# Reading the gate and up products later, behind the next weight tile's split, in a mixture-of-experts stage

## The chip, the core and the metric

The program runs on one core of one Trainium2 chip. The metric is the device time of one execution in microseconds (us), the median of the runs shown; shorter is better. In the profile the core's engines are named PE (matrix products; PEld is its weight load), DVE (element-wise work), ACT (element-wise work with a scale or a function), POOL and SP (which here issues the loads from device memory).

## What is computed

Two layers of a decoder trunk over 272 positions of width 1024, in f32. Each has three token mixers; then layer 0 has a dense SwiGLU block, and layer 1 a mixture of 8 experts, of which every token uses 2. Only the last part is touched here:

```python
def swiglu(h, w_gate, w_up, w_down):
    return (jax.nn.silu(h @ w_gate) * (h @ w_up)) @ w_down

def moe_swiglu(h, router_w, w_gate, w_up, w_down):
    logits = jnp.einsum('btd,de->bte', h, router_w).astype(jnp.float32)
    top_logits, top_idx = lax.top_k(logits, TOP_K)
    ...
    for e in range(N_EXPERTS):
        out = out + combine[..., e:e + 1] * swiglu(h, w_gate[e], w_up[e], w_down[e])
```

The gate and up weights of an expert are 1024 x 3584, the down weights 3584 x 1024, all f32: 44 MB for each expert and 352 MB for the eight.

## The kernel before

The first 850 us or so are the mixers of both layers and the dense block. Then comes the stage of the experts, `experts` (L1162), which is what the change touches.

**Tokens and experts.** The experts are ranked by how many tokens they got. The four fullest are "wide" (up to 128 tokens each), the others "narrow" (up to 64). A token block is gathered by a product with a one-hot matrix (`Group.gather`, L1000) and kept as two parts whose sum is the f32 value: a rounded one and a rest.

**Weights.** An expert is worked through in 7 chunks of 512 hidden columns. A chunk needs 6 loads of 1 MB, in this order: two halves of the gate weights (names r_g), two of the up weights (r_u), two of the down weights (r_d). Every loaded tile is split as a whole (`MoveWeights.parts`, L847): ACT writes the rounded part h_g, h_u or h_d (L855), then DVE the rest, l_g, l_u or l_d (L856). There are 6 raw tiles (`RB`) and 4 pairs of split tiles (`HB`): a load waits until DVE has split the tile six before it, a split waits until PE has used the part four before it. From here on "part" is one such split tile.

**Products.** For each 128 rows of weights a wide expert needs three products of 128 x 512 (L1106 to L1108), a narrow one two (L1134, L1135), since its two halves of tokens stand side by side. A part is 12 products for a wide chunk, 8 for a narrow one. The gate products gather in psg, the up products in psu (two accumulators, `pg`), the down products in y.

**Reading psg and psu.** In a wide chunk ACT reads psg as h (the SiLU, in `act`, L78) and DVE multiplies h by psu (L1113). In a narrow one ACT copies psg to gs (L1140) and psu to us (L1141). Then `turn` brings the result into the layout that the down products need: PE transposes it into hps (L1120, and L1149 for a narrow chunk, gs and us by 8 small products each). In a wide chunk ACT then writes hth (L1124) and DVE htl (L1125). In a narrow one ACT makes s (the SiLU, L78), DVE multiplies it (L1152), and ACT and DVE write ht (L1155, L1156). The down products of a chunk are issued one chunk later: `gate_up` of a chunk, with the `turn` of the chunk before in its middle (`between`), then `down` of the chunk before (`finish`).

**Order.** The list at L1225 to L1231 puts four wide chunks first, then narrow and wide ones by turns, and the three narrow ones that are left last. When an expert's last chunk is done, its sum is weighted (yh, yl) and added to the output (`combine`). SP issues the loads in the order of the program. On the other engines a scheduler sets the order of the instructions: it places each by what it depends on and the estimated times, and the program can add an order between two instructions that share no data (`tc.add_manual_dep` with `nosync`: no wait, only a place behind the other, on the same engine). Each engine then works through its queue strictly in order.

Of the kernel before, what the change touches and what calls it, by code (L numbers as in the profile page):

```python
# [9 lines left out]
F32 = mybir.dt.float32  # L10
# [4 lines left out]
AF = mybir.ActivationFunctionType  # L15
ALU = mybir.AluOpType
# [3 lines left out]
P = 128  # L20
# [31 lines left out]
def trunk(ctx: ExitStack, tc: tile.TileContext, x, meta, n1g, n2g, w_in, qng, kng, dlam,  # L52
# [3 lines left out]
    V, A, G, PE = nc.vector, nc.scalar, nc.gpsimd, nc.tensor  # L56
# [6 lines left out]
    nosync = mybir.DependencyInfo(mybir.DependencyClass.NoSync, mybir.DependencyReason.DATA)  # L63

    def raw_ins(i):
        return getattr(i, "ins", i)
# [9 lines left out]
    def act(*args, **kw):  # L76

        i = raw_ins(A.activation(*args, **kw))  # L78
        for b in phase["before"]:
            tc.add_manual_dep(i, b.name, nosync, reason="tables")  # L80
        phase["now"].append(i)
        return i
# [34 lines left out]
    with ExitStack() as lctx:  # L117
# [16 lines left out]
        def ptile(name):  # L134
            return pm.tile([P, 512], F32, tag="pm", name=name)
# [63 lines left out]
        for k in range(KD):  # L199
            tps = pp.tile([P, 512], F32, tag="pp", name="xT")  # L200
            PE.transpose(tps[:, 0:NM], min_[:, k * P:(k + 1) * P], ident[0:NM, 0:NM])
            for t in range(2):
                c = NM + t * P
# [147 lines left out]
        for l in range(2):  # L351
# [226 lines left out]
            for hp in range(0, NH, 2):  # L578

                lgs = {}  # L580
                for X in (TA, TB):
# [5 lines left out]
                    for m in range(2):  # L587
                        b = m * 2 + hp // 2
                        pss = [ptile("lgps") for _ in range(2)]
# [189 lines left out]
            for fp in range(NFD // 2):  # L779
# [3 lines left out]
                for j in range(2):  # L783
                    pss = []
# [8 lines left out]
                    gs, us, sg = ft[:, 0, :], ft[:, 1, :], ft[:, 2, :]  # L793
# [32 lines left out]
    mo = ctx.enter_context(tc.tile_pool(name="mo", bufs=1, **MT))  # L826
# [7 lines left out]
        return pw.tile([P, 512], F32, tag="pw", name=name)  # L834

    nparts = [0]
    EARLY = 3

    class MoveWeights:
# [7 lines left out]
        def parts(self):  # L847
            st = min(2048 // self.cols, self.nk)
            for k0 in range(0, self.nk, st):
                late = nparts[0] % HB >= HB - LATE  # L850
                wq, nb_ = (wqs[0], LATE) if late else (wqs[1], HB - LATE)
                hi = wq.tile([P, st, self.cols], F32R, tag="hi", bufs=nb_, name="h_" + self.name)
                lo = wq.tile([P, st, self.cols], F32R, tag="lo", bufs=nb_, name="l_" + self.name)
                r = self.raw[:, k0:k0 + st, :]
                ih = raw_ins(A.activation(hi, r, AF.Copy))  # L855
                il = raw_ins(V.tensor_tensor(lo, r, hi.bitcast(F32), op=ALU.subtract))  # L856
                nparts[0] += 1
                if EARLY < nparts[0] < 9:

                    tc.add_manual_dep(il, routed[0].name, nosync, reason="router")  # L860
                if EARLY < nparts[0] < 9:
                    tc.add_manual_dep(ih, last_in[0].name, nosync, reason="router")
                for k in range(st):
                    yield k0 + k, hi[:, k, :], lo[:, k, :]

# [156 lines left out]
    class Expert:  # L1022
# [9 lines left out]
        def gate_up(self, c, between):  # L1032
            pss = []
            for nm, m in (("g", m_wg), ("u", m_wu)):
                ps = pg.tile([P, 512], F32, tag="pg", name="ps" + nm)
                for kh_ in range(2):
                    w = MoveWeights(self.src(m, slice(kh_ * 512, kh_ * 512 + 512), slice(c * 512, c * 512 + 512)),
                                    4, 512, f"{nm}{c}_{kh_}")
                    for kk, hi, lo in w.parts():
                        k = kh_ * 4 + kk  # L1040
                        self.products(ps, [self.g.x[:, k, s] for s in self.sides], hi, lo, k == 0, k == KD - 1)
                pss.append(ps)
                if nm == "g":
                    between()
            return self.gated(*pss)

        def down(self, c, ht):
            if c == 0:
# [52 lines left out]
    class Wide(Expert):  # L1101
# [5 lines left out]
            PE.matmul(ps, st[0], lo, start=False, stop=False)  # L1107
            PE.matmul(ps, st[1], hi, start=False, stop=last)  # L1108

        def gated(self, psg, psu):  # L1110
            h = mo.tile([P, 512], F32, tag="h", bufs=2, name="h")
            act(h, psg, AF.Silu, scale=self.g.ws[:, 0, 1:2])
            V.tensor_tensor(h, h, psu, op=ALU.mult)  # L1113
            return h

        def turn(self, h):

# [10 lines left out]
    class Narrow(Expert):  # L1128
# [5 lines left out]
            PE.matmul(ps, st[0], hi, start=first, stop=False)  # L1134
            PE.matmul(ps, st[0], lo, start=False, stop=last)  # L1135

        def gated(self, psg, psu):
            gs = mo.tile([P, 512], F32, tag="h", bufs=2, name="gs")
            us = mo.tile([P, 512], F32, tag="hu", bufs=2, name="us")
            A.activation(gs, psg, AF.Copy, scale=self.g.ws[:, 1, 1:2])  # L1140
            A.activation(us, psu, AF.Copy)  # L1141
            return gs, us

        def turn(self, gu):
            hps = wtile("hps")
# [16 lines left out]
    def experts(groups, order, first=None):  # L1162


        made, xs = {}, {}
        todo = []

        def group(gi):
            w, n = groups[gi]
            made[gi] = Group(w, n, oh0 if first and gi == 0 else one_hot(w, n, pos_s, sel_s))  # L1170

        def short(n=1):
            for _ in range(min(n, len(todo))):
                todo.pop(0)()

        def finish(x, c, ht):
            if c == NCE - 1:
                ct = x.combine_turn()
            x.down(c, ht)
            if c == NCE - 1:  # L1180
                todo[0:0] = x.combine(ct)

        starts = {}
        for i, (gi, q, kind, c) in enumerate(order):
            starts.setdefault(gi, i)
        group(0)
        for k in range(KD):
            made[0].gather(k)
        if first:
            new_phase("silu_and_others")  # L1190
        prev = None
        for i, (gi, q, kind, c) in enumerate(order):
            for gj, at in starts.items():
                if at == i + (2 if first and gj == 1 else 3):
                    group(gj)
                    todo.extend([lambda g=made[gj], k=k: g.gather(k) for k in range(KD)])
                if at == i and i:
                    short(len(todo))
            if (gi, q) not in xs:
                xs[gi, q] = kind(place[q], made[gi])  # L1200
                xs[gi, q].last = False
            x = xs[gi, q]
            x.last = i == len(order) - 1
            ht = []

            def between():
                if not hasattr(made[gi], "ws"):
                    made[gi].weights()
                short(2 if len(todo) > 4 else 1)
                if prev is not None:  # L1210
                    ht.append(prev[0].turn(prev[2]))
            if first and i == 1:
                residual(1)
            h = x.gate_up(c, between)
            short(2 if len(todo) > 4 else 1)
            if prev is not None:
                finish(prev[0], prev[1], ht[0])
                short()
            prev = (x, c, h)
        finish(prev[0], prev[1], prev[0].turn(prev[2]))  # L1220
        short(len(todo))

# [6 lines left out]
    for i in range(len(narrow)):  # L1229
        order.append(narrow[i])  # L1230
        order.extend(wide[LAG + i:LAG + i + 1])  # L1231
    experts([(0, None)] + [(q, q + WIDE - 1) for q in range(1, WIDE)] + [(None, NE - 1)], order, True)

    cnt = nc.values_load(cmaxi[0:1, 0:1], min_val=0, max_val=S + P // 2)
# [34 lines left out]
```

## Time and profile before

| | us |
|---|---|
| median of 3 runs | 1889.6 |
| lowest and highest run | 1888.64, 1890.66 |
| the profiled execution | 1889.8 |
| its span, first to last instruction | 1888.0 |
| PE busy in the span | 1764.2 (93%) |
| DVE busy | 1438.7 (76%) |
| ACT busy | 1140.0 (60%) |

Busy shares are averages over stages that differ. For the experts one reads the stretch from about 880 us on: first how busy each engine and the DMA engines are there, then which waits there are and what ends them, then the engines' work in order of time for one pair of chunks, a wide one and a narrow one. A wait is idle time of an engine, with the instruction whose end released it. An instruction that waits holds up all that stands behind it in its engine's queue.

### The profile page before, as it was taken

To read this page: it belongs to the slowest core of one execution; us is meant where nothing else is said; L and a number is where in the kernel's file an instruction comes from. 1 tells how busy PE (TensorE), PEld (TensorE's weight loads), DVE (VectorE), ACT (ScalarE), POOL (GpSimd) and SP (SyncE) were. 2 spreads that over 40 slices of the span, in tenths; PEclk is the share of its full clock that TensorE was granted. 3 is DMA by queue.
4 is the path that set the end of the run, shared out by engine and by line. 5 is a ranking of instruction groups with operands and counts; after the bars stand their busy time and mean duration, and the time that the engine had idled before them with its cause. 6 is when DMAs were issued, how large, how long until landed. Compare 5 with 4: busy or idle time off the path is not lost.

```text
span 1888.0 us, 27076 instructions
## 1 busy us (share of the span) xinstructions
PE 1764.2 (93%) x10613; PEld 1523.0 (81%) x10613; DVE 1438.7 (76%) x1600; ACT 1140.0 (60%) x1253; POOL 114.3 (6%) x137
## 2 busy tenths in 40 slices
PE   7999999999999999999998899898899989989986
PEld 7888999999998889998776677676677666767764
DVE  7667657877575776687888788887878878888886
ACT  4376444444443754466776677676677767677765
POOL 5201101000002020020000000000000000000000
PEclk9999999999999999998999999999999999999999
DMA  6333555455553336576999999999999998999994
GB/s 209 100 92 92 179 177 178 158 179 173 174 173 106 109 103 191 187 281 219 342 364 359 314 343 356 344 354 319 343 334 353 359 351 321 356 348 351 365 336 174
DMA packets 266117, 479.91 MB, mean 254 GB/s; under 512 B 7637, under 2 KB 115229, under 8 KB 265981
## 3 DMA queue, kind: packets, MB, share of 16 engines
q1 hardware_dynamic: 265472, 477.20, 72.8%
q8 instruction: 85, 1.39, 0.3%
q0 software_dynamic: 368, 0.86, 0.1%
q14 instruction: 52, 0.42, 0.1%
q10 hardware_dynamic: 140, 0.04, 0.0%
HBM read 477.01 MB, written 1.05 MB: 253 GB/s over the span
## 4 chain that ended last, share of the span: by engine, by line
PE 39%; DVE 14%; ACT 8%; issue 5%; POOL 0%; ACTq 0%; DVEq 0%; POOLq 0%
DVE l_d L856 4%; ACT h_d L855 4%; DVE l_g L856 4%; DVE l_u L856 3%; PE psg L1107 3%; PE psg L1108 2%; PE psg L1106 2%; PE psu L1135 2%; ACT h_g L855 2%; PE y L1107 2%; ACT h_u L855 2%; PE proj L229 2%; PE proj L230 2%; PE proj L228 2%; PE y L1108 2%
## 5 line engine op out<-in xcount | busy, mean ns | idle before, releaser
L856 DVE TENSOR_TENSOR l_d<-r_d,h_d 128x2048 fp32r<-128x2048 f32 (+1 forms) x114 | 256.1, 2250 | 84.8 <-ACT h_d L855 84.8
L230 PE MATMUL proj<-hgh,lo_in 128*128 128x272 f32 (+1 forms) x1024 | 297.5, 291 | 4.6 <-DVE lo_in L224 4.6
L228 PE MATMUL proj<-hgh,hi_in 128*128 128x272 f32 (+1 forms) x1024 | 298.2, 291 | 0.2 <-DVE z L357 0.2
L229 PE MATMUL proj<-hgl,hi_in 128*128 128x272 f32 (+1 forms) x1024 | 296.5, 290 | 0.0
L856 DVE TENSOR_TENSOR l_u<-r_u,h_u 128x2048 fp32r<-128x2048 f32 x112 | 254.6, 2287 | 52.5 <-ACT h_u L855 52.4
L856 DVE TENSOR_TENSOR l_g<-r_g,h_g 128x2048 fp32r<-128x2048 f32 x112 | 255.5, 2286 | 19.0 <-ACT h_g L855 19.0
L223 ACT ACTIVATE hi_in<-raw_in 128x1024 fp32r<-128x1024 f32 x128 | 135.0, 1058 | 166.0 <-PE proj L229 150.6
L855 ACT ACTIVATE h_g<-r_g 128x2048 fp32r<-128x2048 f32 x112 | 213.5, 1910 | 11.6 <-PE psu L1108 6.9
L855 ACT ACTIVATE h_u<-r_u 128x2048 fp32r<-128x2048 f32 x112 | 211.2, 1907 | 12.9 <-PE y L1108 6.5
L855 ACT ACTIVATE h_d<-r_d 128x2048 fp32r<-128x2048 f32 (+1 forms) x114 | 212.3, 1877 | 4.8 <-PE psg L1108 2.5
L230 PEld LDWEIGHTS proj<-hgh,lo_in 128*128 128x128 f32 x1024 | 194.0, 189 | 6.5 <-DVE lo_in L224 5.5
L228 PEld LDWEIGHTS proj<-hgh,hi_in 128*128 128x128 f32 x1024 | 194.1, 190 | 2.8 <-issue 1.1
L229 PEld LDWEIGHTS proj<-hgl,hi_in 128*128 128x128 f32 x1024 | 193.8, 189 | 2.4 <-issue 1.3
L224 DVE TENSOR_TENSOR lo_in<-raw_in,hi_in 128x1024 fp32r<-128x1024 f32 x128 | 158.6, 1241 | 33.8 <-ACT hi_in L223 33.5
L1135 PE MATMUL psg<-l_g,x 128*128 128x512 f32 x224 | 93.8, 419 | 31.0 <-DVE l_g L856 30.8
L1135 PE MATMUL psu<-l_u,x 128*128 128x512 f32 x224 | 95.6, 427 | 28.0 <-DVE l_u L856 27.7
L1107 PE MATMUL y<-l_d,hth 128*128 128x512 f32 x224 | 92.5, 413 | 6.5 <-DVE l_d L856 6.5
L1134 PE MATMUL psu<-h_u,x 128*128 128x512 f32 x224 | 91.1, 407 | 1.5 <-ACT h_u L855 1.5
L1134 PE MATMUL psg<-h_g,x 128*128 128x512 f32 x224 | 89.6, 400 | 1.5 <-ACT h_g L855 1.0
L1107 PE MATMUL psg<-l_g,x 128*128 128x512 f32 x224 | 89.7, 400 | 0.6 <-DVE l_g L856 0.6
L1135 PE MATMUL y<-l_d,ht 128*128 128x512 f32 x224 | 83.7, 405 | 5.9 <-DVE l_d L856 5.7
L1107 PE MATMUL psu<-l_u,x 128*128 128x512 f32 x224 | 88.7, 396 | 0.3
(404 smaller groups left out, 4094.4 us busy)
## 6 DMA issues: line engine op xcount, KB each, us to landing
r_g<-in_moe_w_gate_dram SPq DMA_DIRECT2D x112, 1024.0 KB, 5.9
r_u<-in_moe_w_up_dram SPq DMA_DIRECT2D x112, 1024.0 KB, 7.6
r_d<-in_moe_w_down_dram SPq DMA_DIRECT2D x110, 1024.0 KB, 7.3
raw_in<-in_w_in_dram SPq DMA_DIRECT2D x64, 1024.0 KB, 5.9
raw_br<-in_w_branch_dram SPq DMA_DIRECT2D x12, 1024.0 KB, 5.4
raw_fg<-in_ffn_w_gate_dram SPq DMA_DIRECT2D x11, 1024.0 KB, 5.4
raw_fu<-in_ffn_w_up_dram SPq DMA_DIRECT2D x11, 1024.0 KB
raw_wo<-in_w_out_dram SPq DMA_DIRECT2D x8, 1024.0 KB, 4.9
```

The source lines that it names most:

```text
L223: A.activation(hi, r, AF.Copy)
L224: V.tensor_tensor(lo, r, hi.bitcast(F32), op=ALU.subtract)
L228: PE.matmul(ps, sh, mh, start=first, stop=False)
L229: PE.matmul(ps, sh, ml, start=False, stop=False)
L230: PE.matmul(ps, sl, mh, start=False, stop=last)
L855: ih = raw_ins(A.activation(hi, r, AF.Copy))
L856: il = raw_ins(V.tensor_tensor(lo, r, hi.bitcast(F32), op=ALU.subtract))
L1106: PE.matmul(ps, st[0], hi, start=first, stop=False)
L1107: PE.matmul(ps, st[0], lo, start=False, stop=False)
L1108: PE.matmul(ps, st[1], hi, start=False, stop=last)
L1134: PE.matmul(ps, st[0], hi, start=first, stop=False)
L1135: PE.matmul(ps, st[0], lo, start=False, stop=last)
```

## The change

The function `gated`, which read psg and psu at the end of `gate_up`, is taken apart. `hold` makes the tile for the result, `gated_g` reads psg and `gated_u` reads psu. Both are put on a list, `behind`, with a count of 1, and run when the next weight part has been split, with an added order that places them behind it: behind ACT's half of the split (`ih`) for the reads on ACT, behind DVE's half (`il`) for the wide chunk's product with psu. `gated_g` goes on the list behind the up products, so that it follows the next part, which is the first down part of the chunk before. `gated_u` goes on it after those down products, so that it follows the first gate part of the next chunk. What is left at the end is run at once.

```diff
     nparts = [0]
+    behind = []
     EARLY = 3
...
                     tc.add_manual_dep(ih, last_in[0].name, nosync, reason="router")
+                for b in list(behind):
+                    b[0] -= 1
+                    if b[0] == 0:
+                        behind.remove(b)
+                        x_ = b[1]()
+                        tc.add_manual_dep(x_, (il if b[2] else ih).name, nosync, reason="behind")
                 for k in range(st):
                     yield k0 + k, hi[:, k, :], lo[:, k, :]
...
                 if nm == "g":
                     between()
-            return self.gated(*pss)
+            h = self.hold()
+            behind.append([1, lambda: self.gated_g(h, pss[0]), False])
+            return h, pss[1]
...
-        def gated(self, psg, psu):
-            h = mo.tile([P, 512], F32, tag="h", bufs=2, name="h")
-            act(h, psg, AF.Silu, scale=self.g.ws[:, 0, 1:2])
-            V.tensor_tensor(h, h, psu, op=ALU.mult)
-            return h
+        def hold(self):
+            return mo.tile([P, 512], F32, tag="h", bufs=2, name="h")
+
+        def gated_g(self, h, psg):
+            return act(h, psg, AF.Silu, scale=self.g.ws[:, 0, 1:2])
+
+        def gated_u(self, h, psu):
+            return raw_ins(V.tensor_tensor(h, h, psu, op=ALU.mult))
...
-        def gated(self, psg, psu):
-            gs = mo.tile([P, 512], F32, tag="h", bufs=2, name="gs")
-            us = mo.tile([P, 512], F32, tag="hu", bufs=2, name="us")
-            A.activation(gs, psg, AF.Copy, scale=self.g.ws[:, 1, 1:2])
-            A.activation(us, psu, AF.Copy)
-            return gs, us
+        def hold(self):
+            return (mo.tile([P, 512], F32, tag="h", bufs=2, name="gs"),
+                    mo.tile([P, 512], F32, tag="hu", bufs=2, name="us"))
+
+        def gated_g(self, h, psg):
+            return raw_ins(A.activation(h[0], psg, AF.Copy, scale=self.g.ws[:, 1, 1:2]))
+
+        def gated_u(self, h, psu):
+            return raw_ins(A.activation(h[1], psu, AF.Copy))
...
-            h = x.gate_up(c, between)
+            h, psu = x.gate_up(c, between)
             short(2 if len(todo) > 4 else 1)
             if prev is not None:
                 finish(prev[0], prev[1], ht[0])
                 short()
+            behind.append([1, lambda x=x, h=h, psu=psu: x.gated_u(h, psu), kind is Wide])
             prev = (x, c, h)
+        for b in behind:
+            b[1]()
+        behind.clear()
```

The change is written in the order of the program, and the scheduler carries it over to the queues. On ACT, in a narrow chunk in the middle of the stage and the start of the wide chunk after it, there stands before (the names are those of the program with running numbers; _0 and _1 or _2 are a chunk's first and second tile of a kind):

```order
L855 ACTIVATE h_u_0_11108<-r_u_0_11106 128x2048
L1140 ACTIVATE gs<-psg,ws 128x512
L855 ACTIVATE h_u_1_11122<-r_u_1_11120 128x2048
L855 ACTIVATE h_d_0_11142<-r_d_0_11140 128x2048
L1141 ACTIVATE us<-psu 128x512
L855 ACTIVATE h_d_2_11160<-r_d_2_11158 128x2048
L78 ACTIVATE s<-hps 128x256
L855 ACTIVATE h_g_0_11179<-r_g_0_11177 128x2048
L1155 ACTIVATE ht<-s 128x4x64
L855 ACTIVATE h_g_1_11197<-r_g_1_11195 128x2048
L855 ACTIVATE h_u_0_11231<-r_u_0_11229 128x2048
```

The read of psg stands between the two up parts, the read of psu between the two down parts, and hth two rows above the first row shown. Now there stands at the same place on ACT:

```order
L856 ACTIVATE h_u_0_11108<-r_u_0_11106 128x2048
L1136 ACTIVATE hth<-hps 128x512
L856 ACTIVATE h_u_1_11122<-r_u_1_11120 128x2048
L856 ACTIVATE h_d_0_11140<-r_d_0_11138 128x2048
L1154 ACTIVATE gs<-psg,ws 128x512
L856 ACTIVATE h_d_2_11159<-r_d_2_11157 128x2048
L856 ACTIVATE h_g_0_11178<-r_g_0_11176 128x2048
L1157 ACTIVATE us<-psu 128x512
L856 ACTIVATE h_g_1_11197<-r_g_1_11195 128x2048
L78 ACTIVATE s<-hps 128x256
L856 ACTIVATE h_u_0_11231<-r_u_0_11229 128x2048
L1170 ACTIVATE ht<-s 128x4x64
```

gs has moved behind h_u_1 and h_d_0, us behind h_d_2 and the next chunk's h_g_0; hth, s and ht, which the program did not move, stand one or two parts later as well.

On DVE, between a wide chunk and the narrow chunk after it (l is the rest of a split, h the product with psu), there stands before:

```order
L1113 TENSOR_TENSOR h<-h,psu 128x512
L856 TENSOR_TENSOR l_d_2_11056<-r_d_2_11053,h_d_2_11055 128x2048
L856 TENSOR_TENSOR l_g_0_11071<-r_g_0_11068,h_g_0_11070 128x2048
L1125 TENSOR_TENSOR htl<-hps,hth 128x512
L856 TENSOR_TENSOR l_g_1_11085<-r_g_1_11082,h_g_1_11084 128x2048
L856 TENSOR_TENSOR l_u_0_11109<-r_u_0_11106,h_u_0_11108 128x2048
L856 TENSOR_TENSOR l_u_1_11123<-r_u_1_11120,h_u_1_11122 128x2048
```

The product stands between the two down parts, htl between the two gate parts. Now, on DVE at the same place:

```order
L857 TENSOR_TENSOR l_d_2_11055<-r_d_2_11052,h_d_2_11054 128x2048
L857 TENSOR_TENSOR l_g_0_11070<-r_g_0_11067,h_g_0_11069 128x2048
L1126 TENSOR_TENSOR h<-h,psu 128x512
L857 TENSOR_TENSOR l_g_1_11085<-r_g_1_11082,h_g_1_11084 128x2048
L857 TENSOR_TENSOR l_u_0_11109<-r_u_0_11106,h_u_0_11108 128x2048
L1137 TENSOR_TENSOR htl<-hps,hth 128x512
L857 TENSOR_TENSOR l_u_1_11123<-r_u_1_11120,h_u_1_11122 128x2048
```

The product has moved two parts later, behind the next chunk's l_g_0, and htl with it, behind l_u_0. On PE the transposes into hps move from the middle of the second down part to the first products of the second gate part.

## Rows read from the trace of the kernel before

**Rows 1.** Window: start:end, length; engines busy (instructions), PE clock, DMA share, GB/s.

```profile
1000.00:1800.00 800.00, 725.73 (x3243) 559.93 (x3242) 660.89 (x427) 560.44 (x437) 0.00 (x0) 0.99 0.96 345
```

**Rows 2.** Waits, 1000 to 1800: us in total, times, longest us.

```profile
DVE l_d L856 <- ACT h_d L855: 68.9, 38, 3.5
ACT hth L1124 <- PE hps L1120: 51.2, 22, 3.4
ACT us L1141 <- PE psu L1135: 48.9, 19, 3.8
ACT gs L1140 <- PE psg L1135: 47.2, 18, 4.0
...
ACT h L78 <- PE psg L1108: 32.2, 19, 2.0
```

**Rows 3.** Timelines of ACT, DVE, PE in a plain pair: start, us, what, idle before.

```profile
1731.04 0.69 ACT L1140 ACTIVATE gs<-psg,ws 128x512 f32<-128x512 f32 x1 [2.70 <-PE psg L1135]
1731.62 1.90 ACT L855 ACTIVATE h_u<-r_u 128x2048 fp32r<-128x2048 f32 x1
...
1733.56 2.29 DVE L856 TENSOR_TENSOR l_u<-r_u,h_u 128x2048 fp32r<-128x2048 f32 x1 [2.30 <-ACT h_u L855]
...
1735.91 0.51 PE L1135 MATMUL psu<-l_u,x 128*128 128x512 f32 x1 [1.13 <-DVE l_u L856]
...
1766.11 0.69 ACT L1140 ACTIVATE gs<-psg,ws 128x512 f32<-128x512 f32 x1 [2.95 <-PE psg L1135]
```

**Rows 4.** Timeline of ACT: further reads of psg, one per narrow chunk.

```profile
997.44 0.69 ACT L1140 ACTIVATE gs<-psg,ws 128x512 f32<-128x512 f32 x1 [1.02 <-PE psg L1135]
...
1801.17 0.69 ACT L1140 ACTIVATE gs<-psg,ws 128x512 f32<-128x512 f32 x1 [2.68 <-PE psg L1135]
...
1858.30 0.69 ACT L1140 ACTIVATE gs<-psg,ws 128x512 f32<-128x512 f32 x1 [2.64 <-PE psg L1135]
```

**Rows 5.** Windows of two pairs (the second a plain one) and two short stretches.

```profile
971.61:1004.22 32.61, 30.45 (x145) 24.61 (x144) 27.53 (x16) 21.69 (x17) 0.00 (x0) 1.00 1.02 382
1766.11:1801.17 35.06, 31.97 (x143) 24.42 (x142) 28.64 (x17) 25.18 (x19) 0.00 (x0) 1.00 0.99 359
824.00:844.00 20.00, 20.00 (x176) 19.84 (x174) 15.87 (x21) 17.32 (x28) 6.77 (x6) 1.00 1.05 387
975.00:1000.00 25.00, 23.96 (x118) 19.57 (x117) 19.92 (x14) 16.58 (x14) 0.00 (x0) 1.00 1.04 395
```

**Rows 6.** DMA issues of r_u, 1000 to 1800: KB each, median us from issue to landing.

```profile
r_u<-in_moe_w_up_dram SPq DMA_DIRECT2D x87, 1024.0 KB, 7.6
```

**Rows 7.** Timeline of PE: products back to back, and the transposes of both kinds.

```profile
1317.13 0.40 PE L1108 MATMUL psu<-h_u,x 128*128 128x512 f32 x1
...
1321.26 0.39 PE L1108 MATMUL psu<-h_u,x 128*128 128x512 f32 x1
...
1723.49 0.60 PE L1120 MATMUL hps<-ident,h 128*128 128x128 f32 x4
...
1738.49 1.10 PE L1149 MATMUL hps<-ii,us 128*128 128x64 f32 x8 [0.23 <-ACT us L1141]
```

**Rows 8.** Timeline of ACT in the first two pairs, 939 to 1005.

```profile
939.44 0.59 ACT L1141 ACTIVATE us<-psu 128x512 f32<-128x512 f32 x1
...
961.52 3.73 ACT L855 ACTIVATE h_u<-r_u 128x2048 fp32r<-128x2048 f32 x2 [2.02 <-PE y L1134]
...
966.96 0.67 ACT L1140 ACTIVATE gs<-psg,ws 128x512 f32<-128x512 f32 x1
...
971.61 0.59 ACT L1141 ACTIVATE us<-psu 128x512 f32<-128x512 f32 x1
...
978.19 1.92 ACT L855 ACTIVATE h_u<-r_u 128x2048 fp32r<-128x2048 f32 x1 [2.26 <-DMA r_u<-in_moe_w_up_dram]
...
995.81 0.60 ACT L1124 ACTIVATE hth<-hps 128x512 fp32r<-128x512 f32 x1 [2.44 <-PE hps L1120]
...
1004.22 0.60 ACT L1141 ACTIVATE us<-psu 128x512 f32<-128x512 f32 x1 [2.50 <-PE psu L1135]
```

## The prediction, made before the changed kernel was run

> **What bounds the kernel now.** I read first where the time lies. From 880 us on the program streams expert weights, and no engine is full there: of the 800 us from 1000 to 1800 PE is busy 725.7, DVE 660.9, ACT 560.4, and the DMA engines move 345 GB/s [rows 1]. So I asked next who waits for whom. Three of ACT's waits are for a finished product of PE: us 48.9 us, gs 47.2 us and h 32.2 us, together 128.3 us in 800 [rows 2]. Each is read once in a pair of one wide and one narrow chunk, and the stretch holds 22 pairs (800 us at 36.5, below): 5.8 us a pair. What stands behind those reads on ACT is the next tile's split: DVE idles 68.9 us for h_d alone [rows 2], and PE in its turn stands still for 74.3 us [rows 1]. This is a ring: ACT waits for PE, DVE for ACT, PE for DVE. The reader can watch one turn of it [rows 3]: ACT waits 2.70 us and reads gs at 1731.04, only then splits h_u at 1731.62, DVE has idled 2.30 us for it and starts l_u at 1733.56, and PE stands 1.13 us before 1735.91.
>
> The length of a pair is read from gs to gs: 1731.04 to 1766.11 to 1801.17, 35.1 us each where nothing else is to be done, and 997.44 to 1801.17 over 22 pairs, 36.53 us on average [rows 3, 4]. The excess of 1.4 us is what gathers and combines of the experts add.
>
> Is DMA the bound? In the plain pair from 1766.11 it moves 359 GB/s [rows 5], and 12 tiles of 1.049 MB (12.58 MB) in 35.1 us are just that. But its engines are not at their limit: with up to six loads queued it moved 387 GB/s for 20 us (824 to 844), and 395 GB/s for 25 us (975 to 1000) [rows 5]. Also, a load of r_u lands 7.6 us after its issue [rows 6], so at one tile per 3.0 us only two or three of six raw tiles are in flight. The others lie loaded and wait for the split. DMA follows; it doesn't lead.
>
> **The change part by part.** It adds and removes no instruction: the same reads, later in their queues. The loads' order on SP is the same.
>
> *gs, us and h move behind a further split.* In the order shown, ACT now splits h_u_1 and h_d_0 before gs, and h_d_2 and h_g_0 of the next chunk before us; a wide chunk's h comes after h_d_0, and DVE's product with psu after the next l_g_0. When does PE finish what they read? Take hth's read as zero, with PE at the first product of psg's second part. PE's products step by 0.23 us (18 steps between 1317.13 and 1321.26 [rows 7]). So psg ends at 1.6 us (7 products). ACT comes to gs at 0.6 + 2 x 1.9 = 4.4 us, with 0.60 for hth [rows 8] and 1.9 for a split [rows 3]. Then psu: 16 products take 3.7 us, but PE must wait for the split of u1 (below), so it ends near 6.6; ACT comes to us at 4.4 + 0.7 + 2 x 1.9 = 8.9. The wide chunk's h has two full splits more ahead of it than psg has products left. So ACT's 5.8 us go, and the ring is open at these three places. The same move takes DVE's product away from the end of psu.
>
> *What is late next.* Two reads of ACT stay close behind PE: hth (51.2 us now [rows 2]) and s. hth moves from behind h_g_0 to behind h_u_0. If ACT gets there first, it starts h_u_1 only after PE's transposes; 0.6 + 1.9 + 2.3 (the split on DVE) = 4.8 us later l_u_1 is there, while PE has 15 products, 3.4 us. This is a stall of 1.4 us per pair. s moves to behind h_g_1, and PE has 23 products (5.3 us) against 0.4 + 1.9 + 2.3 = 4.6: no stall. So PE would need 120 products of 0.23 (27.5), transposes of 0.6 and 2 x 1.1 [rows 7] and 1.4: about 31.7 us, 33.1 with the 1.4 for gathers and combines. The busy time of PE gives the other bound: 725.7 us in 22 pairs [rows 1], 33.0 with gathers, combines and no stall.
>
> *DMA as the next bound.* 12.58 MB at 387 GB/s are 32.5 us, at 395 they are 31.9. DVE needs 660.9 us of 800 now [rows 1], 30.2 us a pair; ACT less.
>
> *Is there a pair of the kernel before that ran in the new order?* Yes, and this is the row on which I rely most. In the first narrow chunks the scheduler happened to put u, u, d ahead of gs, as at 966.96 (behind the two splits of h_u from 961.52 and one of h_d), and there ACT doesn't wait for it [rows 8]. From us to us these pairs take 32.2 and 32.6 us (939.44, 971.61, 1004.22) [rows 8]. At 978.19 ACT even waits 2.26 us for the load of r_u [rows 8], which it does nowhere from 1000 to 1800, and DMA moves 382 GB/s in the second of them [rows 5]. So the new order gives about 32.4 us with DMA next in line.
>
> *The sum.* A pair: 32.4 us, and half of the 1.4 us for gathers and combines, since work that DMA covers is free: 33.1. I choose half between nothing (32.4, all hidden) and all of it (33.8). Saved: 22 x (36.53 - 33.1) = 75 us. The three narrow chunks at the end (gs from 1801.17 to 1858.30, 19.0 us each [rows 4]) become 17.0: six tiles at 387 GB/s are 16.25, and half of the 1.4 again; 6 us. Before 997 the order hardly differs in effect, and behind the last load nothing changes: 0. Together 81 us. The profiled execution took 1889.8 us with a span of 1888.0, 0.2 over the median of 1889.6: 1889.6 - 81 = 1808.6 us.
>
> *A rule against it.* The row comes first: 387 and 395 GB/s for 20 and 25 us [rows 5]. The Trainium skill, page "DMA: Bandwidth & Descriptors", section "Where 436 GB/s comes from", says that a transfer from HBM to SBUF is bound on the HBM side, at about 358 GB/s per core. By that rule a plain pair would already be at its floor, and the first rival below would be the result. The same page, section "Bandwidth", reports 425 GB/s for 16 MB with the other core of the pair idle, as here; the trace's 387 and 395 GB/s side with that.
>
> **Rivals.**
>
> *DMA caps at what a plain pair shows.* If 387 to 395 GB/s is a burst (the longest stretch seen is 25 us), pairs stay at 35.1 us and only the surplus goes: 22 x 1.4 = 31, and 3 x 1.4 at the end: 1854 us. For it: the plain pair from 1766.11 has a DMA share of 0.99 [rows 5]. Against it: the landing after 7.6 us [rows 6], and that ACT waits for no load in 1000 to 1800. I give 10%.
>
> *The waits move to hth and s, and gathers are not hidden.* Then PE's ring sets the pair: 33.1 with one stall of 1.4; with a second such stall, at a combine or at s, 34.5. 22 x 2.0 = 45 and 3 at the end: 1842 us. For it: hth's wait is the longest of ACT's now, and its place is near PE still. Against: the fast pairs, one of which had a wait of 2.44 us for hth [rows 8]. 19%, with 1825 to 1846.
>
> *Slower: the turn of the hidden activations comes late.* The transposes of h now stand behind psg's next part on PE, because DVE multiplies only after l_g_0. If hth, htl, s and ht, each behind one split more, come later than PE's down products, PE stalls a split of 2.2 us on DVE in each chunk: 2 x 2.2 + 1.4 = 5.8 us a pair. PE's idle time to win back is 3.4 us a pair (800 - 725.7 over 22 [rows 1]), so from there on the pair grows, to 36.53 + 2.4: 1889.6 + 53 = 1943 us. It decides only if the slack between htl (1.3 us after zero) and PE's first down product (6.6) is used up, some 5 us. 5%.
>
> *No effect*, DMA or another place holding 36.5 us: 1890, 3%.
>
> **How the numbers follow.** Forecast case (pairs of 32.4 to 33.8; all hidden: 22 x 4.13 + 3 x 2.8 = 99, 1790 us; none: 22 x 2.73 + 3 x 1.4 = 64, 1825 us): 60%. Pairs below 32.4, down to DMA's 31.9 (1780 us): 3%. Second rival 19%, first 10%, slower 5%, no effect 3%. The range of 8 in 10 is 1786 to 1846: the forecast, the second rival and the better half of the faster pairs; left out are 1854 and above, no effect and slower, 18%, and a little below 1786. A measurement tells 0.2% from no change: faster 0.92, same 0.03, slower 0.05.
>
> **What would show it.** In the profile of the changed kernel: ACT's waits for psg and psu below 15 us in 1000 to 1700 (128.3 now); waits of ACT's splits for loads, which are absent now; DMA at 375 to 390 GB/s; loads landing 9 to 12 us after issue; DVE's wait for h_d below 30 us; gs to gs about 33 us; the last load some 80 us earlier. Wrong would be: gs and us without waits, but hth and s with twice theirs and DMA below 360 GB/s (second rival); or ACT waiting for loads at 360 GB/s (first rival).

## The result: 1800.1 us, and the profile of the changed kernel

The changed kernel took 1800.13 us (median of 4 runs, 1799.28 to 1801.32) beside 1889.18 us for the kernel before on the same chip: a ratio of 0.9528, with a 95% interval from 0.9511 to 0.9544. The prediction was 1809 in a range of 1786 to 1846. The span of the profiled execution fell from 1888.0 to 1797.5 us, by 90.5.

The page of the changed kernel first: busy time of each engine, its share of the span, instructions. PE's busy time fell by 36.8 us, with the same number of instructions; that of the other engines is within 6 us of before, in a shorter span.

```profile
PE 1727.4 (96%) x10613; PEld 1520.7 (85%) x10613; DVE 1436.3 (80%) x1600; ACT 1134.6 (63%) x1253; POOL 114.5 (6%) x137
```

The window of the experts, 1000 to 1700 us (it answers to [rows 1]; the streaming ends some 90 us earlier now): length, busy us of PE, PEld, DVE, ACT and POOL with instructions, PE clock, DMA share, GB/s.

```profile
1000.00:1700.00 700.00, 673.02 (x3136) 542.20 (x3136) 635.97 (x414) 536.40 (x423) 0.00 (x0) 1.00 1.02 380
```

DMA moves 380 GB/s where it moved 345 [rows 1], and PE stands still for 27 us in 700 where it stood for 74 in 800. (Windows of 700 and 800 us are compared here and below; where it matters, the value of before for the same 700 us is given too.) Then the waits of the same 700 us (it answers to [rows 2]): us in total, times, longest.

```profile
ACT s L78 <- PE hps L1164: 66.5, 21, 4.4
ACT hth L1136 <- PE hps L1132: 41.8, 19, 3.0
...
DVE l_u L857 <- ACT h_u L856: 18.7, 16, 1.4
PE psu L1147 <- DVE l_u L857: 17.2, 24, 1.7
...
PE psg L1147 <- DVE l_g L857: 7.4, 9, 1.4
...
DVE l_d L857 <- ACT h_d L856: 5.7, 5, 1.4
```

The reader is to look for what is missing. us, gs and h, 128.3 us in [rows 2], have no row that ends on PE, nor further down the answer. DVE's wait for h_d, 68.9 us there (60.1 in the same 700 us), is 5.7. What ACT still waits for is the two reads that the program did not move: hth at 41.8 us, and s at 66.5. In the kernel before these two stood, in the same 700 us, at

```profile
ACT hth L1124 <- PE hps L1120: 45.1, 19, 3.4
...
ACT s L78 <- PE hps L1149: 13.0, 5, 4.3
```

So ACT's waits moved to s alone; hth's are about what they were. The answer for ACT alone shows the waits for loads, which [rows 2] does not have:

```profile
ACT h_g L856 <- DMA r_g<-in_moe_w_gate_dram: 1.7, 3, 0.8
ACT h_u L856 <- DMA r_u<-in_moe_w_up_dram: 1.5, 3, 0.8
```

Together 3.2 us in 700: the loads are nearly never late. One plain pair on ACT, with the one PE stall in it (it answers to [rows 3]): start, us, what, and in brackets the idle time before it.

```profile
1656.24 0.60 ACT L1136 ACTIVATE hth<-hps 128x512 fp32r<-128x512 f32 x1 [1.76 <-PE hps L1132]
1656.74 1.91 ACT L856 ACTIVATE h_u<-r_u 128x2048 fp32r<-128x2048 f32 x1
...
1660.34 0.68 ACT L1154 ACTIVATE gs<-psg,ws 128x512 f32<-128x512 f32 x1
...
1661.47 0.50 PE L1147 MATMUL psu<-l_u,x 128*128 128x512 f32 x1 [0.69 <-DVE l_u L857]
...
1664.52 0.59 ACT L1157 ACTIVATE us<-psu 128x512 f32<-128x512 f32 x1
...
1670.85 0.38 ACT L78 ACTIVATE s<-hps 128x256 f32<-128x256 f32 x1 [3.93 <-PE hps L1164]
...
1691.90 0.68 ACT L1154 ACTIVATE gs<-psg,ws 128x512 f32<-128x512 f32 x1
```

gs and us are read without a wait. From gs to gs the pair takes 31.6 us (35.1 before [rows 3]). The wait of 1.76 us for hth stands ahead of h_u, and PE's one stall, 0.69 us, is at that part's l_u. The wait of 3.93 us for s has no PE stall behind it. In this pair DMA moves 394 GB/s (the line answers to the second one of [rows 5]):

```profile
1660.34:1691.90 31.56, 30.65 (x142) 24.57 (x141) 29.01 (x17) 24.69 (x19) 0.00 (x0) 1.00 1.04 394
```

The ends of the 22 pairs and of the program, on ACT (it answers to [rows 4]):

```profile
996.06 0.68 ACT L1154 ACTIVATE gs<-psg,ws 128x512 f32<-128x512 f32 x1
...
1723.24 0.68 ACT L1154 ACTIVATE gs<-psg,ws 128x512 f32<-128x512 f32 x1
...
1771.68 0.67 ACT L1154 ACTIVATE gs<-psg,ws 128x512 f32<-128x512 f32 x1
...
1774.72 0.60 ACT L1157 ACTIVATE us<-psu 128x512 f32<-128x512 f32 x1 [2.37 <-PE psu L1147]
```

From 996.06 to 1723.24 these are 727.2 us, 33.05 a pair; before, 803.7 and 36.53. So of the 90.5 us, 76.5 lie in the 22 pairs. The three narrow chunks at the end took 57.1 us [rows 4] and take 48.4: 8.7. Up to the third gs it is 1.4. The rest behind the last gs, 29.7 and now 25.8, is 3.9, but there the mark itself has moved: gs is read later in the chunk. From the last us, which before was this row on ACT,

```profile
1865.08 0.60 ACT L1141 ACTIVATE us<-psu 128x512 f32<-128x512 f32 x1 [2.22 <-PE psu L1135]
```

to the end of the span it is 22.9 us before (1888.0 - 1865.08) and 22.8 now (1797.5 - 1774.72): nothing.

### The profile page after: what moved, and what is told of

Its sections match the earlier page's. It is cut to its first block, busy times and chain, and to the rows that moved or that the text cites. A ratio compares the mean times of both kernels' runs of the same rounds, so it can differ in the third digit from the quotient of the medians.

```text
span 1797.5 us, 27073 instructions
## 1 busy us (share of the span) xinstructions
PE 1727.4 (96%) x10613; PEld 1520.7 (85%) x10613; DVE 1436.3 (80%) x1600; ACT 1134.6 (63%) x1253; POOL 114.5 (6%) x137
## 4 chain that ended last, share of the span: by engine, by line
PE 47%; DVE 11%; issue 4%; ACT 3%; POOL 0%; DVEq 0%; ACTq 0%; POOLq 0%
DVE l_u L857 5%; PE y L1116 3%; PE y L1117 3%; PE y L1115 3%; PE psg L1116 3%; PE psg L1115 3%; PE psg L1117 3%; PE psu L1115 2%; PE psu L1116 2%; PE psu L1117 2%; PE hps L1164 2%; PE proj L229 2%; PE proj L228 2%; PE proj L230 2%; PE psu L1147 2%
## 5 line engine op out<-in xcount | busy, mean ns | idle before, releaser
L856 ACT ACTIVATE h_g<-r_g 128x2048 fp32r<-128x2048 f32 x112 | 213.7, 1914 | 17.5 <-PE psu L1117 12.5
L224 DVE TENSOR_TENSOR lo_in<-raw_in,hi_in 128x1024 fp32r<-128x1024 f32 x128 | 158.7, 1241 | 34.0 <-ACT hi_in L223 33.7
L1115 PE MATMUL psu<-h_u,x 128*128 128x512 f32 x224 | 88.6, 396 | 0.0
L1146 PE MATMUL psu<-h_u,x 128*128 128x512 f32 x224 | 88.5, 395 | 0.0
```

## Experiments

The theory, called A in the expectations, is the ring of the prediction: a read by ACT close behind the PE products that make its input holds up ACT's next split, that DVE's, and that PE. Each of the two reads should then be worth a part of the gain. Rival B puts the gain on the later hth and s, which come along when the reads of psu are put off; rival C puts it on the reads of psu themselves. Later runs set A against a bound by DMA. All ratios are against the kernel before on the same chip. "Gain" is that kernel's time there less the run's.

### One read at a time

Only the read of psg is put off; psu is read behind it at the old place.

```diff
-            behind.append([1, lambda: self.gated_g(h, pss[0]), False])
+            behind.append([1, lambda: (self.gated_g(h, pss[0]), self.gated_u(h, pss[1]))[0], False])
...
-            behind.append([1, lambda x=x, h=h, psu=psu: x.gated_u(h, psu), kind is Wide])
```

> Only the reads of psg move behind the next down part's split; psu is read right behind them, which is where it was read before (ACT: u0, u1, d0, gs, us, d2; hth stays behind g0, as before). Theory A (each read of ACT that follows PE closely costs PE its own stall, and the stalls add up): the stall at l_u of 2.0 us a plain pair goes, those at l_g (1.6), l_d (1.1 and 1.1) stay, so a plain pair takes 33.1 us instead of 35.1 and the whole 1840 to 1855 us. Rival B (what helped is that the scheduler moved hth and s one or two parts later as well): hth and s stand as before, so 1880 to 1890 us. Rival C (only psu's reads matter, as the last ones of a chunk): 1880 to 1890 us too.

Measured: 1837.64 us (1836.92 to 1838.33), ratio 0.9732 [0.9716, 0.9748], 2.4 us below the range of A.

Only the read of psu is put off:

```diff
-            behind.append([1, lambda: self.gated_g(h, pss[0]), False])
+            self.gated_g(h, pss[0])
             return h, pss[1]
```

> Only the reads of psu move behind the next gate part; psg is read as soon as may be (ACT: u0, hth, gs, u1, d0, d2, g0, us). Theory A: hth and gs now stand together one part behind PE, gs waits for the end of psg 1.6 us after the transposes, so l_u comes 1.6 us later than in the changed kernel and a plain pair takes 33.0 us instead of 31.4: 1830 to 1845 us in all. Rival B (hth and s have moved here as in the changed kernel, and that is what helped): 1798 to 1805 us. Rival C (psu's reads alone matter): 1798 to 1810 us.

Measured: 1835.87 us (1835.07 to 1836.29), ratio 0.972 [0.9704, 0.9737].

Each alone gains a little over half of the whole, 51 and 53 us; B and C fall as causes of the whole (a part of B comes back below, in htl). Where PE stalls says more than the totals. The rows are PE's waits for a split part in narrow chunks, 1000 to 1700 us. The kernel before:

```profile
PE psg L1135 <- DVE l_g L856: 24.3, 33, 1.6
PE psu L1135 <- DVE l_u L856: 20.5, 18, 1.8
```

With the read of psg alone put off:

```profile
PE psg L1147 <- DVE l_g L857: 22.7, 33, 1.5
...
PE psu L1147 <- DVE l_u L857: 4.4, 8, 1.0
```

With the read of psu alone put off:

```profile
PE psu L1147 <- DVE l_u L857: 25.8, 23, 1.8
...
PE psg L1147 <- DVE l_g L857: 8.6, 14, 1.4
```

Before, the read of psg stood between the two up parts on ACT; put off, it takes away PE's wait for l_u. The read leaves its place, and the stall goes at the part that was queued behind it. The wait for l_g is another matter: it has its place on DVE. Where the wide chunk's product with psu is not put off, DVE writes htl between the next chunk's two gate parts, here with the read of psg alone put off:

```profile
1683.48 2.29 DVE L857 TENSOR_TENSOR l_g<-r_g,h_g 128x2048 fp32r<-128x2048 f32 x1
1685.68 0.68 DVE L1137 TENSOR_TENSOR htl<-hps,hth 128x512 fp32r<-128x512 f32 x1
1686.28 2.28 DVE L857 TENSOR_TENSOR l_g<-r_g,h_g 128x2048 fp32r<-128x2048 f32 x1
```

Put off, it takes the transposes and with them htl to the next pair of parts, here in the changed kernel:

```profile
1687.22 2.29 DVE L857 TENSOR_TENSOR l_u<-r_u,h_u 128x2048 fp32r<-128x2048 f32 x1
1689.42 0.69 DVE L1137 TENSOR_TENSOR htl<-hps,hth 128x512 fp32r<-128x512 f32 x1
1690.24 2.29 DVE L857 TENSOR_TENSOR l_u<-r_u,h_u 128x2048 fp32r<-128x2048 f32 x1
```

In a narrow chunk PE is through a part in 8 products of 0.23 us, 1.8 us, while DVE needs 2.3 us for the next; with 0.7 us of htl between two parts PE runs dry. ACT's wait for hth, which stands at the same place, is not the cause: in the rows above l_u starts 0.13 us after the end of htl, and in none of the 21 pairs from 1000 to 1700 us of the changed kernel does DVE idle for h_u there. In the kernel before the stall at l_g was htl's and the one at l_u was the read's. With the read of psu alone put off both are at l_u: 25.8 us (there DVE does idle for h_u behind htl, up to 1.7 us, since ACT reads hth and gs ahead of it). In the changed kernel the read has left, and 17.2 us remain; how much of that is htl's is tested below.

### One kind of chunk at a time

The reads are put off in narrow chunks alone, then in wide ones alone.

```diff
-            behind.append([1, lambda: self.gated_g(h, pss[0]), False])
+            if isinstance(self, Wide):
+                self.gated_g(h, pss[0])
+                self.gated_u(h, pss[1])
+            else:
+                behind.append([1, lambda: self.gated_g(h, pss[0]), False])
...
+            if kind is not Wide:
+                behind.append([1, lambda x=x, h=h, psu=psu: x.gated_u(h, psu), False])
```

The second kernel has the same edit with the two kinds exchanged.

> Only narrow chunks read psg and psu later; wide chunks read both where they did before (the SiLU ahead of d0, the product with psu between l_d of the two down parts, and so hth behind g0). Theory A: gs and us hold nothing up, but l_g still comes 1.6 us late (hth behind g0) and l_d 1.1 us late (the product waits for the end of psu); a plain pair takes some 33.5 us, the whole 1838 to 1855 us, the narrow chunks at the end as short as in the changed kernel. A rival by which only ACT's 96 us of waits for gs and us count, not their places: 1805 to 1820 us.

Measured: 1826.22 us (1825.22 to 1827.19), ratio 0.9668 [0.9652, 0.9685], a gain of 62 us, more than expected. The narrow chunks at the end are those of the changed kernel (14.3 and 14.6 us for the last two).

> Only wide chunks read psg and psu later; narrow ones read both as soon as may be (ACT: u0, hth, gs, u1, d0, us, d2). Theory A: the stall at l_d of the wide chunk's product (1.1 us) and the one at l_g (1.6, since hth moves) go, the one at l_u grows to 3.0 and the one at l_d behind us (1.1) stays; a plain pair takes 33.5 to 34.5 us and the whole 1840 to 1868 us; the narrow chunks at the end take 17 to 19 us each, as before. The rival by which only gs and us count: 1880 to 1890 us.

Measured: 1848.5 us (1847.32 to 1850.32), ratio 0.979 [0.9774, 0.9807], a gain of 40 us.

PE's waits again, narrow chunks alone:

```profile
PE psg L1151 <- DVE l_g L857: 22.9, 33, 1.6
...
PE psu L1151 <- DVE l_u L857: 5.5, 9, 1.1
```

and wide chunks alone:

```profile
PE psu L1151 <- DVE l_u L857: 25.3, 23, 1.7
...
PE psg L1151 <- DVE l_g L857: 5.5, 8, 1.2
```

The same pattern: with narrow chunks alone htl is still between the gate parts and the stall at l_g is the old one; with wide chunks alone htl has moved, and both stalls are at l_u. So the wide half of the change did part of its work by moving htl, an instruction that it does not name.

The four runs also set single reads against each other, as each kernel puts off two of the four. gs and us gain 62 us, gs and the wide h 51: us is worth 11 more than h. The wide product with psu gains 53 us with us and 40 with h: again us is worth more, by 13. The halves add up to 104 us (psg and psu) and 101 (narrow and wide), and both together gain 89: the first half takes away something that the second would have, too. Which wait that is was not settled.

### The two reads left over: hth, then s

hth and htl are put behind one split more:

```diff
-            A.activation(hth, ps3, AF.Copy)
-            V.tensor_tensor(htl, ps3, hth.bitcast(F32), op=ALU.subtract)
-            return hth, htl
+            def read():
+                i = raw_ins(A.activation(hth, ps3, AF.Copy))
+                V.tensor_tensor(htl, ps3, hth.bitcast(F32), op=ALU.subtract)
+                return i
+
+            behind.append([2, read, False])
+            return hth, htl
...
```

> The changed kernel with hth and htl of a wide chunk one part later, behind u1 instead of u0. Theory A: the stall of 1.0 to 1.4 us a pair that PE still has at l_u goes, a plain pair takes 30.3 us and the whole 1772 to 1785 us. Rival D (with 12.58 MB a pair in 31.4 us, 401 GB/s, DMA is the bound of the changed kernel): no change, 1796 to 1804 us, and ACT begins to wait for loads.

Measured: 1791.61 us (1790.52 to 1793.87), ratio 0.9485 [0.9469, 0.9501]. A pair takes 32.76 us on average. PE's wait:

```profile
PE psu L1151 <- DVE l_u L857: 6.1, 6, 1.7
```

It falls from 17.2 to 6.1 us in 700, 0.5 us a pair or 11.5 in 22; 8.5 us are gained. On DVE htl now stands behind the second up part. So most of the stall that the changed kernel has left in the up products was that of hth and htl. The gain is between the two expectations: the stall goes, but less than A's whole price comes out. As D expected, ACT's waits for loads grow, from 3.2 to 16.5 us in 700. In the last kernel s and ht are put off as well, in the same way with a count of 1:

> As the run with hth late, and s and ht of a narrow chunk one part later too, behind u0 instead of g1. Theory A: s holds up ACT by 3 us a pair but PE by 0.3 us at most, so 0 to 8 us less than with hth alone late. Rival D (DMA bound): the same time as the changed kernel, 1796 to 1804 us. A third possibility: ht now comes too late for the down products, PE waits there, and the time is 5 to 30 us over that with hth alone late.

Measured: 1786.07 us (1783.78 to 1788.1), ratio 0.9461 [0.9445, 0.9477]; and once more, in another comparison:

> The kernel of e4_both_late word for word, beside e9_yh_late on the same chip, so that a difference of a few us between the two can be told: 1783 to 1789 by every theory.

Measured: 1788.14 us (1787.65 to 1789.67), ratio 0.9473 [0.9457, 0.9489]. This kernel is faster than both, by 12 to 14 us against the changed one. ACT's waits in it, 1000 to 1700 us:

```profile
ACT s L78 <- PE hps L1168: 37.7, 17, 4.4
...
ACT h_u L856 <- DMA r_u<-in_moe_w_up_dram: 13.6, 21, 1.1
ACT hth L1137 <- PE hps L1132: 11.6, 9, 3.0
ACT h_g L856 <- DMA r_g<-in_moe_w_gate_dram: 10.7, 19, 0.8
```

The waits for s and hth, 108.3 us in the changed kernel, are 49.3, and the waits for loads have gone from 3.2 to 24.3. As the waits for PE go, ACT comes to the loads.

### Are the loads the next bound?

To each 1 MB load of that last kernel a load of 64 KB is added, into a tile that nobody reads: 1/16 more bytes.

```diff
             nc.sync.dma_start(self.raw, src)
+            nc.sync.dma_start(wx.tile([P, 1, 128], F32, tag="wx", name="wx"), src[:, 0:1, 0:128])
...
```

> The kernel with hth and s late, and behind each weight load one more load of 64 KB into a tile that nothing reads: 6.25% more bytes, 13.37 MB a pair, order on ACT and DVE nearly the same. If DMA has become the bound (its best 20 us show 393 to 397 GB/s), a pair takes 34.0 us instead of 32.6 and the whole 1812 to 1828 us, with ACT waiting for loads. If PE's ring is still the bound, nothing changes: 1782 to 1792 us.

Measured: 1847.33 us (1846.99 to 1847.94), ratio 0.9782 [0.9766, 0.9798], about 61 us more than without the added loads. The rate in 40 slices of 1000 to 1700 us, first with the added loads:

```profile
GB/s 385 386 385 386 386 385 386 386 386 386 386 386 386 385 386 386 383 386 386 386 386 386 385 381 386 386 386 385 386 386 373 383 385 386 384 381 332 368 381 386
```

and without them, in the kernel that this one was made from:

```profile
GB/s 394 395 358 384 396 394 392 391 340 351 392 390 393 393 393 391 389 395 396 393 393 372 330 390 388 393 394 393 392 394 394 394 395 394 386 349 384 392 393 393
```

With the added loads nearly every slice stands at 386: a ceiling. ACT now waits for loads:

```profile
ACT h_g L858 <- DMA r_g<-in_moe_w_gate_dram: 41.2, 43, 1.9
...
ACT h_u L858 <- DMA r_u<-in_moe_w_up_dram: 35.4, 42, 1.7
```

A plain pair takes 34.6 us, and 12 tiles with their additions, 13.37 MB, at 386 GB/s are 34.6 us. This kernel is bound by its loads; they land 11.2 to 11.3 us after issue, where they took 8.2 to 9.4 without the additions. The cost was above the expectation, since the ceiling also fell, from about 394 to 386. The kernel without the added loads reaches its ceiling of 392 to 396 in most slices and falls to 330 to 358 in five. At 394, 12.58 MB take 31.9 us, its mean pair 32.57. So in the fastest kernel the loads are next in line: by this estimate 0.6 us a pair is left above them.

The other way: the second up tile is not loaded, and the first is split twice (1/6 of the bytes left out).

```diff
...
-                                    4, 512, f"{nm}{c}_{kh_}")
+                                    4, 512, f"{nm}{c}_{kh_}", w.raw if kh_ and nm == "u" else None)
...
```

> The kernel with hth and s late, but the second tile of the up weights is not loaded: the first one's tile is split a second time in its place. A sixth of the bytes is left out, the rest of the work stays (the product with the up weights is wrong). The scheduler, which counts on earlier loads, places hth behind gs and s later. If DMA is the bound with hth and s late: a pair falls to PE's own 31.7 us (30.3 and the 1.4 for gathers and combines) and the whole to 1760 to 1774 us. If not: 1782 to 1790 us.

Measured: 1795.19 us (1793.88 to 1795.71), ratio 0.9503 [0.9487, 0.9519]: 7 to 9 us slower than the two runs with all loads, with fewer bytes. DMA moves 320 GB/s from 1000 to 1700 us, and the longest of ACT's waits, 29.1 us ahead of h_g, is for split tiles that PE still uses. But this is no clean test: the scheduler, which sees the load times, put hth behind gs and s elsewhere, and with the marks moved pairs read from gs to gs came out between 27.4 and 42.5 us, plain ones at 31.4. It says one thing only: with the loads out of the way a plain pair took 31.4 us. Whether the same order with fewer bytes would be faster stays open.

### One read more

Pairs with a combine are longer than plain ones, and there ACT waits for yh, the finished sum. Its first read is put one split later (edit: `behind.append([2, ready, False])`, with `ready` doing what `prepare(0)` did at once).

> The kernel of e4_both_late with one more read given a lead: the first read of a finished expert's sum by ACT (yh, at three pairs in four of the combine) stands behind the second gate part g1 instead of the first, so one split part more lies between it and the product that it waits for. Theory A (a lead of one split part pays wherever ACT waits for PE): in the kernel after, between 1000 and 1700 us, ACT waits 11.3 + 11.2 us for yh in its six reads there; if half of that goes in the whole span, 3 to 14 us less than e4_both_late, 1772 to 1783. Theory D (with ACT's waits for loads at 24.3 us of 700 and DMA at 386 GB/s the loads are the next in the ring, so a lead only turns a wait for PE into a wait for a load): within 4 us of e4_both_late, 1782 to 1790, with ACT's waits for loads longer by about what yh lost.

Measured: 1792.29 us (1789.36 to 1792.37), ratio 0.9488 [0.9472, 0.9504], beside 1788.14 without the edit. That is 4 us more, just outside what theory D allowed; A is out. In the narrow experts' combines the waits for yh are those without the edit (2.71, 2.71 and 3.88 us; 2.71, 2.71 and 3.90). In the wide experts' combines ACT's wait at the moved read fell, but a new one came behind it, at the second read, which had none. ACT without the edit, at the first combine of the stretch:

```profile
1036.28 0.69 ACT L1087 ACTIVATE yh<-y,ws 128x512 fp32r<-128x512 f32 x1 [4.06 <-PE y L1117]
```

and with it:

```profile
1038.35 0.69 ACT L1088 ACTIVATE yh<-y,ws 128x512 fp32r<-128x512 f32 x1 [2.03 <-PE y L1124]
...
1042.48 0.69 ACT L1088 ACTIVATE yh<-y,ws 128x512 fp32r<-128x512 f32 x1 [1.63 <-PE sc L1096]
```

The second read is now the one that comes too early. Over 700 us the waits for yh are 17.1 us (17.3 without), and hth's rose from 11.6 to 17.3 us. ACT's waits for loads did not grow (17.1 after 25.6 for gate and up): it is not the loads that ate it. Why hth lost as much was not followed up.

## Why the prediction was right, and where it was right by luck

**The ring.** Right, and shown: the waits for us, gs and h are gone, DVE's for h_d fell to 5.7 us, and PE's wait for l_u fell from 20.5 us to 4.4 and 5.5 where the narrow chunks' read of psg was put off and htl left in its place, and stood at 25 us where htl moved and that read did not. With both, as in the changed kernel, it is 17.2. What the ring did not say is that the other stall, at l_g, was htl's work on DVE; it went because the change carried htl along. The rival "no effect" and the slower one are out: s and hth come later, and PE's down products don't wait for them: PE has no row for y left in the 700 us, neither for hth (0.4 us before) nor for a split down part (5.3 us in wide chunks and 3.2 in narrow ones before).

**The first rival, and the rule for it.** DMA does not stop at 359 GB/s: it moved 380 over 700 us. The Trainium skill ("DMA: Bandwidth & Descriptors", section "Where 436 GB/s comes from") has the HBM side bind at about 358 GB/s. The trace of before sided against that rule for 25 us; the one of the changed kernel does for 700, and the kernel with added loads held 386 in nearly every slice. No run reached the 425 GB/s of the same page's section "Bandwidth".

**The plain pair: 32.4 predicted, 31.3 to 31.6 measured.** The step that failed is "the new order gives about 32.4 us". It took the first pairs of the kernel before as a floor, although they held a wait of 2.44 us for hth and one of 2.26 us for a load [rows 8]. The second of them did not run in the new order either: ACT waits 1.02 us for gs at 997.44 [rows 4] and 2.50 us for us at 1004.22 [rows 8]. The PE ledger in the paragraph before, 31.7 us, was the better row: 120 products, the transposes and one stall. Its stall was sized at 1.4 us and put on ACT's wait for hth; the measured waits for l_u, 17.2 us over the 21 pairs in 700 us, are 0.8, most of it from htl on DVE (6.1 us are left once hth and htl are put off). The other bound of that paragraph, PE's busy time of 33.0 us a pair, was no floor: the 673.02 us of the window over its 21.2 pairs are 31.8, and in the whole program the same 10613 instructions of PE took 36.8 us less. Why they did was not followed up (the mean granted clock is 0.990 before and 0.997 now). DMA did not set the pair: ACT waits 3.2 us for loads in 700, and loads land 7.4 to 9.3 us after issue, not 9 to 12. But it was nearer than these waits say, and so "with DMA next in line" was not wrong: the 394 GB/s of the plain pair is what the kernel with hth and s late has for a ceiling. The issues of the changed kernel, KB each and median us to landing (they answer to [rows 6]):

```profile
r_d<-in_moe_w_down_dram SPq DMA_DIRECT2D x85, 1024.0 KB, 7.4
r_g<-in_moe_w_gate_dram SPq DMA_DIRECT2D x85, 1024.0 KB, 9.3
r_u<-in_moe_w_up_dram SPq DMA_DIRECT2D x84, 1024.0 KB, 8.1
```

A plain pair of 31.4 us is even shorter than 12 tiles need at 394 GB/s (31.9), the shortest pair that a case of the prediction counts with: in 31.56 us 12.43 MB arrive where 12.58 are split, so it lives on tiles that landed during the longer pairs.

**Gathers and combines: 0.7 us a pair predicted, 1.65 measured** (33.05 - 31.4). This is the same error seen from the other side. Half was to be hidden behind DMA; but with PE 96% busy its own extra products are on the path, by what the trace shows (no run leaves them out). The nine of the 22 pairs that are over 33 us long take 35.4 us on average, and PE is busy 33.7 of them; in the plain pair above it is busy 30.65 of 31.56. So some 3 of the 4 us more are PE's own. The groups of PE for them in the 700 us: busy us, mean ns, idle before.

```profile
L1012 PE MATMUL gat<-oh,hnl 128*128 128x192 f32 (+1 forms) x48 | 10.5, 273 | 0.0
L1095 PE MATMUL sc<-yh,ct 128*128 128x512 f32 x24 | 9.4, 433 | 0.3
L1012 PE MATMUL gat<-oh,hnh 128*128 128x192 f32 (+1 forms) x48 | 8.8, 259 | 0.0
L1096 PE MATMUL sc<-yl,ct 128*128 128x512 f32 x24 | 8.2, 403 | 0.5 <-DVE yl L1088 0.5
```

They sum to 36.9 us, 1.74 for each of some 21 pairs, the size of what was measured. The two errors are -1.0 and +0.95 us a pair and cancelled: 33.05 beside the predicted 33.1, 76.5 us beside 75. That the pairs came out so close was luck.

**The second rival** was half right: ACT's waits did move to s (from 13.0 to 66.5 us in 700; those for hth, 45.1, fell to 41.8), and gathers were not hidden. Its price was wrong. At s the wait cost little, as the ledger of the prediction said (23 products against 4.6 us): putting s off as well brought 3 to 6 us; at hth and htl the stall was at most 0.8 us, not 1.4 and a second such one.

**The tail.** 8.7 us for the three narrow chunks where 6 was predicted: 18 tiles at 387 GB/s are 48.8 us, and 48.4 was measured, at 389 GB/s. The sum of that term was right; the addition for gathers and combines, 0.7 us for each, had no place there. For a single chunk it does not hold: the last two take 14.3 and 14.6 us, less than the 16.25 of six tiles, and ACT waits for no load in the three. DVE is busy 45.29 of the 48.44 us; which of the two sets the time was not tested. Behind the last us: 0, as predicted. The remaining 1.4 us come before the third gs. The sum, 76.5 + 8.7 + 3.9 + 1.4, with the 3.9 us of the moved mark, is 90.5, 9 us beyond the 81 predicted.

## What to carry to other kernels

When engines work strictly in order and form a ring, no engine is full and the waits look harmless one by one; put a read of an accumulator one whole work item behind the products that make it, look for the gain at the item that was queued behind the read, and list every instruction that moves with it: small work between two halves of a feed costs as much as a wait. It paid here for gs, us, h and htl, where the part behind the read was one that PE soon ran out of; for s it brought little, for yh nothing. Price such changes by a ledger of the engine that closes the ring, its products times their step with the stalls added; pairs of the old kernel that still hold waits are no floor, nor is the engine's busy time in them, and side work is only free while another engine is the bound. Once the waits for PE are gone the next one is near: here the loads, 0.6 us a pair away.

## What had not been expected of the hardware

In these kernels the load rate has a ceiling that depends on what is loaded: about 394 GB/s in 17.5 us slices with loads of 1 MB alone, and a flat 386 where a 64 KB load stands beside each. 6.25% more bytes cost 2.4 us on 32.57 a pair, 7.3%. Whether it is the number of the loads or the shape of the small ones (128 rows of 512 bytes) was not tried.
